# The last down projection by token tiles, with the final norm behind each tile

## The chip, the cores and the metric

The kernel runs on one core of one Trainium2 chip. The core has five engines that work side by side and wait for one another by semaphores: TensorE (PE; its weight loads are listed as PEld), VectorE (DVE), ScalarE (ACT), GpSimd (POOL) and SyncE (SP, which only issues transfers). Products are accumulated in PSUM, which has eight banks of 128 partitions by 512 float32. All else lies in SBUF. The metric is the device time of one execution in microseconds, as the median of several.

## The reference, cut to what matters

The program is a trunk of four layers over 512 tokens of width 1024. Each layer adds a mixer (S5, gated linear attention, differential attention, S5 again) and then a feed-forward part to the residual stream `x`; a last norm gives the output. The change concerns the last lines only:

```python
def rmsnorm(x, g):
    xf = x.astype(jnp.float32)
    y = xf * lax.rsqrt(jnp.mean(xf * xf, axis=-1, keepdims=True) + NORM_EPS)
    return (y * g.astype(jnp.float32)).astype(x.dtype)

def swiglu_ffn(h, w_gate_up, w_down):
    g, u = jnp.split(h @ w_gate_up, 2, axis=-1)
    return (jax.nn.silu(g) * u) @ w_down
...
        h = rmsnorm(x, norm_ffn[layer])
        x = x + swiglu_ffn(h, w_gate_up[layer], w_down[layer])
    return rmsnorm(x, norm_final)
```

The hidden width of the feed-forward part is 2816, which the kernel handles as eleven blocks of 256.

## The kernel before, in words

**Tiles.** `x` lies in SBUF as 128 partitions by four token tiles by 1024 columns. All products run in float32r, and each operand is split into a high part (a rounded copy) and a low part (the rest), so that one product of 128 x 128 by 128 x 512 is three matmuls: high by high, high by low, low by high. That is `mm3` (L394), whose three matmuls are L396, L397 and L398.

**Weights.** One panel of the down weights is 256 rows by 512 columns, 512 KB. `wb` (L388) loads it through SP's queue into one of three staging buffers `wst` (L357), ACT copies the high part into one of five split buffers `whl` (L368), and DVE writes the low part behind it (L376).

**The feed-forward part.** `ffn` (L717) works on the eleven blocks in three groups of 4, 4 and 3 (L799). For each block, gate and up products are made, gated and split into `act` (L704, L705). After each group the group's share of the down product is added to `x`. In the last group that is six row blocks k of 128 hidden columns, so three panels for each of the two column halves d.

**The down product.** `gemm_b` (L400) takes one half at a time. It opens four accumulators in PSUM (tag `acc`, four banks), one for each token tile, and goes over panels, over the two row blocks in a panel and over the four token tiles. When a tile's last k is done, `add_x` (L539) scales the bank by the token's norm factor `r` and adds it to `x` on DVE (L548). For half 1 of the last group the last four k (`tail=4`) are taken token tile by token tile, so that the four sums end one behind the other. PSUM's other four banks are two of tag `s` and two of tag `tp`, which the last group's down product does not use.

**The final norm.** `run` (L2486) ends with a loop over the token tiles. `normed` (L492) lets ACT square a tile of 1024 columns into a scratch tile `sq` and sum it along the way (L500), DVE adds epsilon (L487), POOL raises to the power -1/2 (L489), and DVE multiplies the tile by that factor and by the gain into a tile `h` (L504), which SP stores (L2508). `sq` and `h` have two buffers each and come from a pool `last`, opened when the feed-forward part's pool has been closed. The gain comes by a load on SP's queue (L480) into the one buffer of tag `gain`, which the feed-forward part lends out as a room for weights before.

**What sets the order.** A first stretch of each feed-forward part is ordered by hand (L749 to L785). From L786 on, a planner orders each engine's instructions: it goes by the order in the program and by its own estimate of when operands and buffers are ready, and it writes all waits. Within an engine the order it gave is fixed at run time. `issue_after` ties an instruction behind another one of the same engine; `gemm_b` uses it, by way of `self.behind`, so that in half 0 of a group's down product the panels behind the first are split only after the last silu on ACT and the last scaling on DVE (L367, L372, L835).

Of the kernel before, what the change touches and what calls it, by code (L numbers as in the profile page):

```python
# [11 lines left out]
F32 = mybir.dt.float32  # L12
# [3 lines left out]
AF = mybir.ActivationFunctionType  # L16
ALU = mybir.AluOpType
# [4 lines left out]
P = 128  # L22
D = 1024
SEQ = 512
NT = SEQ // P
# [14 lines left out]
class Slices:  # L40
# [5 lines left out]
    @staticmethod  # L46
    def flat(t):
        dims = "abcdef"[: len(t.shape) - 1]
        return t[:] if len(dims) == 1 else t[:].rearrange(f"p {' '.join(dims)} -> p ({' '.join(dims)})")
# [239 lines left out]
class Trunk:  # L289
# [199 lines left out]
        nc.gpsimd.tensor_tensor(r[:], v, self.mhalf[:, :n], op=ALU.pow)  # L489
        return r  # L490

    def normed(self, xt, g, out, pool, aside=False):  # L492

        nc = self.nc
        if pool is None:
            junk = self.wp.tile([P, D], F32, tag="wst", name="sq", bufs=3)
        else:
            junk = pool.tile([P, D], F32, tag="sq", name="sq", bufs=2)
        ms = self.sp.tile([P, 1], F32, tag="ms", name="ms", bufs=2)
        nc.scalar.activation(junk[:], xt, AF.Square, scale=1.0 / 32.0, accum_out=ms[:])  # L500
        r = self.rsqrt(ms[:], 1, 1e-6)
        if out is None:
            h = pool.tile([P, D], F32, tag="h", name="h", bufs=2)
            nc.vector.scalar_tensor_tensor(h[:], xt, r[:], g[:], op0=ALU.mult, op1=ALU.mult)  # L504
            return h
        if aside:
            nc.scalar.mul(junk[:], xt, r[:])
            gr = lambda y: y.rearrange("p (g c) -> p g c", c=16)
            nc.gpsimd.tensor_tensor(out, gr(junk[:]), gr(g[:]), op=ALU.mult)
            return  # L510
        nc.vector.scalar_tensor_tensor(
            out, xt.rearrange("p (g c) -> p g c", c=16), r[:],
            g[:].rearrange("p (g c) -> p g c", c=16), op0=ALU.mult, op1=ALU.mult,
        )

    def split_t(self, dst_hi, dst_lo, src):
        nc = self.nc
        nc.scalar.copy(dst_hi, src)
        nc.vector.tensor_tensor(dst_lo, src, dst_hi.bitcast(F32), op=ALU.subtract)
# [50 lines left out]
    def seven_block(self, fp, slots, left, wgu, b, turn, na):  # L570
# [143 lines left out]
            add, six, six_out, seven, seven_out, three, three_out, four, gate2, parts, four_out,  # L714
        )}

    def ffn(self, l, left, after=None, turn=False, aside=None, small=None):  # L717


        jobs = bool(aside or small)  # L720
        i = self.i
        wgu, wd = i["ffn_w_gate_up"][l], i["ffn_w_down"][l]
        nxt = None
        r = left.r
        with self.tc.tile_pool(name=f"ffn{l}", bufs=1, reuse_waits="tile") as fp:
# [13 lines left out]
            f = blocks[:2]  # L739
# [27 lines left out]
            for step in plan.split():  # L767
                name, _, n = step.partition(":")
# [12 lines left out]
                elif name == "turn":  # L781
                    r = self.turn_x(left.r) if turn else r
# [15 lines left out]
            b0 = 0  # L798
            for nb in (4, 4, 3) if na == 4 else (3, 3, 3, 2):  # L799
                acts = []  # L800
                for n in range(b0, b0 + nb):
                    b = blocks[n]
                    if n > 1:
                        for w in ("direct", "room1", "room22", "room21", "summed"):
                            b[w]()
                    if n < 2:
                        b["gate2"]()
                        continue
                    if n == 2:
                        b["one"]()  # L810
                        b["five"]()
                        b["one_out"]()
                        b["add"]("22")
                        b["split"]("1")
                        b["split"]("21")
                        acts.append(blocks[0]["parts"]())
                        acts.append(blocks[1]["parts"]())
                        b["five_out"]()
                    else:
                        for step in ("one", "one_out", "five", "five_out"):  # L820
                            b[step]()
                        b["add"]("22")
                    if n > 1:
                        for step in ("six", "six_out", "two", "two_out", "gate1", "seven", "seven_out", "three", "three_out"):
                            b[step]()
                        b["add"]("21")
                        b["four"]()
                    acts.append(b["four_out"]())
                stat = lambda k, part, t: acts[k // 2][:, part, k % 2, t * P : (t + 1) * P]
                if b0 + nb == 11 and after is not None:  # L830
                    nxt = (Chunks if turn else Left)(self, after)
                for d in range(2):
                    tail = 4 if d == 1 and b0 + nb == 11 else 0
                    self.gemm_b(stat, wd, 2 * nb, d * 512, self.add_x(d, nxt, r), k0=2 * b0, tail=tail, jobs=jobs,
                                behind=None if d else dict(self.last))  # L835
                b0 += nb
# [1340 lines left out]
    def diff(self, l, left):  # L2177
# [4 lines left out]
        with self.tc.tile_pool(name="diff", bufs=1) as p:  # L2182
# [193 lines left out]

            units = project(0, 0)
            run(units)
            tables()
            units = project(0, 1)  # L2380
            run(units)
            units = project(0, 2)
            run(units, 8)
            rest()
            prepare(0)
# [100 lines left out]
    def run(self):  # L2486
        nc, i = self.nc, self.i
        with ExitStack() as ctx:
            left = self.s5_first(ctx)

        def small():
            yield from self.diff_tables()
            yield from self.s5_phases_spilled(1)

        left = self.ffn(0, left, i["norm_mix"][1], aside=lambda fp: self.s5_spilled(fp, 1))
        left = self.gla(1, left)
        left = self.ffn(1, left, i["norm_mix"][2], small=small)
        left = self.diff(2, left)
        left = self.ffn(2, left, i["norm_mix"][3], turn=True)
        with ExitStack() as ctx:  # L2500
            left = self.s5_second(3, ctx, left)
        self.ffn(3, left)
        g = self.gain(i["norm_final"])
        o = self.out[0].rearrange("(p t) c -> p t c", t=NT)
        with self.tc.tile_pool(name="last", bufs=1, side="right") as p:
            for t in range(NT):
                h = self.normed(self.x[:, t], g, None, p)
                nc.sync.dma_start(o[:, t], h[:])  # L2508


_INS = [
# [35 lines left out]
```

## Time and profile before

| | |
|---|---|
| median of 3 runs | 2273.04 us (2271.74 to 2274.02) |
| profiled execution | 2275.95 us, its span 2274.2 us |
| TensorE busy | 2208.0 us, 97% of the span |
| DVE, ACT, POOL busy | 1560.9, 1120.4, 281.0 us |
| granted TensorE clock, mean | 0.991 |
| first matmul of the last down product | starts at 2228.24 us |
| last matmul of the program | starts at 2260.66 us |

The span runs from the first to the last instruction on the core; the profiled execution's time is a little more. Times in the timeline are microseconds from the span's start. A row of the timeline gives start, duration, engine, line, operation, output and inputs, shape, and in brackets how long the engine stood idle before it and who released it. A row of the groups by line gives count, busy time and mean nanoseconds. SPq is SP's queue of transfer issues. Matmuls overlap one another, so a matmul's own duration is longer than the step from one to the next.

### The profile page before, as it was taken

To read this page: it belongs to the slowest core of one execution; us is meant where nothing else is said; L and a number is where in the kernel's file an instruction comes from. 1 tells how busy PE (TensorE), PEld (TensorE's weight loads), DVE (VectorE), ACT (ScalarE), POOL (GpSimd) and SP (SyncE) were. 2 spreads that over 40 slices of the span, in tenths; PEclk is the share of its full clock that TensorE was granted. 3 is DMA by queue.
4 is the path that set the end of the run, shared out by engine and by line. 5 is a ranking of instruction groups with operands and counts; after the bars stand their busy time and mean duration, and the time that the engine had idled before them with its cause. 6 is when DMAs were issued, how large, how long until landed. Compare 5 with 4: busy or idle time off the path is not lost.

```text
span 2274.2 us, 37228 instructions
## 1 busy us (share of the span) xinstructions
PE 2208.0 (97%) x14847; PEld 1959.7 (86%) x14847; DVE 1560.9 (69%) x2420; ACT 1120.4 (49%) x1870; POOL 281.0 (12%) x392
## 2 busy tenths in 40 slices
PE   6999999999999999999999999999999899999997
PEld 4778989889777799998988887999998888989896
DVE  8873977776624469777744675977766964957574
ACT  6533645454453455555535676644444234635342
POOL 1000141522000010101002231101000001101000
PEclk9999999999999999999999999999999999999999
DMA  4247476663422457766336366976631646767521
GB/s 86 50 145 193 107 195 161 174 189 90 123 68 72 138 141 188 188 165 172 97 126 147 90 150 156 242 208 148 171 90 46 159 130 158 194 159 181 152 76 65
DMA packets 295463, 317.83 MB, mean 140 GB/s; under 512 B 72221, under 2 KB 235353, under 8 KB 294906
## 3 DMA queue, kind: packets, MB, share of 16 engines
q1 hardware_dynamic: 233050, 234.23, 34.3%
q0 software_dynamic: 62240, 81.22, 19.2%
q8 instruction: 117, 1.92, 0.3%
q14 instruction: 56, 0.46, 0.1%
HBM read 283.54 MB, written 16.65 MB: 132 GB/s over the span
## 4 chain that ended last, share of the span: by engine, by line
PE 81%; DVE 9%; ACT 4%; issue 2%; DMA 2%; SPq 1%; POOL 0%; ACTq 0%; DVEq 0%; POOLq 0%
PE a L565 18%; PE acc L396 13%; PE acc L398 13%; PE acc L397 13%; PE c L565 8%; PE d L565 4%; PE y L1481 2%; DVE whl L376 2%; ACT whl L368 1%; PE V L1445 1%; PE s L2309 1%; PE op L2343 1%; PE tp L123 1%; DVE halves L229 1%; ACT halves L211 1%
## 5 line engine op out<-in xcount | busy, mean ns | idle before, releaser
L376 DVE TENSOR_TENSOR whl<-wst,whl 128x1024 fp32r<-128x1024 f32 x272 | 331.8, 1224 | 262.9 <-ACT whl L368 262.3
L368 ACT CAST whl<-wst 128x1024 fp32r<-128x1024 f32 x272 | 284.0, 1050 | 312.6 <-PE acc L398 220.8
L565 PE MATMUL a<-side,whl 128*128 128x256 f32 x3168 | 383.0, 277 | 3.9 <-DVE whl L376 3.6
L565 PEld LDWEIGHTS a<-side,whl 128*128 128x128 f32 x3168 | 369.6, 188 | 6.5 <-DVE whl L376 5.5
L396 PE MATMUL acc<-whl,act 128*128 128x512 f32 x704 | 278.3, 396 | 0.8 <-DVE x L548 0.7
L397 PE MATMUL acc<-whl,act 128*128 128x512 f32 x704 | 274.7, 390 | 0.0
L398 PE MATMUL acc<-whl,act 128*128 128x512 f32 x704 | 274.6, 390 | 0.0
L565 PE MATMUL c<-side,whl 128*128 128x256 f32 x2112 | 254.7, 277 | 1.2 <-DVE whl L376 1.2
L565 PEld LDWEIGHTS c<-side,whl 128*128 128x128 f32 x2112 | 247.0, 188 | 2.0 <-DVE whl L376 2.0
L376 DVE TENSOR_TENSOR whl<-slot,whl 128x1024 fp32r<-128x1024 f32 x107 | 130.5, 1223 | 68.7 <-ACT whl L368 68.7
L396 PEld LDWEIGHTS acc<-whl,act 128*128 128x128 f32 x704 | 132.1, 188 | 31.1 <-issue 2.3
L398 PEld LDWEIGHTS acc<-whl,act 128*128 128x128 f32 x704 | 132.2, 188 | 28.1
L397 PEld LDWEIGHTS acc<-whl,act 128*128 128x128 f32 x704 | 132.2, 188 | 25.6
L368 ACT CAST whl<-slot 128x1024 fp32r<-128x1024 f32 x107 | 112.2, 1053 | 82.4 <-PE acc L398 34.1
L396 PE MATMUL acc<-whl,hT 128*128 128x512 f32 x352 | 142.8, 406 | 0.0
L398 PE MATMUL acc<-whl,hT 128*128 128x512 f32 x352 | 138.2, 393 | 0.0
L397 PE MATMUL acc<-whl,hT 128*128 128x512 f32 x352 | 138.0, 392 | 0.0
L565 PE MATMUL a<-sides,whl 128*128 128x256 f32 x1056 | 134.3, 283 | 0.0
L565 PEld LDWEIGHTS a<-sides,whl 128*128 128x128 f32 x1056 | 129.8, 191 | 0.9
L565 PE MATMUL d<-sides,whl 128*128 128x256 f32 x1056 | 126.6, 276 | 1.0 <-ACT whl L368 1.0
L565 PEld LDWEIGHTS d<-sides,whl 128*128 128x128 f32 x1056 | 122.9, 188 | 1.2 <-ACT whl L368 1.2
L704 ACT CAST act<-r 128x512 fp32r<-128x512 f32 (+1 forms) x110 | 66.3, 646 | 116.0 <-DVE r L683 108.5
(458 smaller groups left out, 3884.1 us busy)
## 6 DMA issues: line engine op xcount, KB each, us to landing
wst<-in_ffn_w_gate_up_dram SPq DMA_DIRECT2D x88, 512.0 KB, 4.9
wst<-in_ffn_w_down_dram SPq DMA_DIRECT2D x88, 512.0 KB, 4.3
slot<-in_ffn_w_gate_up_dram SPq DMA_DIRECT2D x71, 512.0 KB, 5.6
wst<-in_ffn_w_gate_up_dram POOLq DMA_DIRECT2D x44, 512.0 KB, 6.2
halves<-in_ffn_w_gate_up_dram SPq DMA_DIRECT2D x43, 512.0 KB, 5.3
wst<-in_s_w_glu_dram SPq DMA_DIRECT2D x32, 512.0 KB, 4.6
wst<-in_gla_w_in_dram SPq DMA_DIRECT2D x24, 512.0 KB, 3.8
wst<-in_diff_w_qkv_dram SPq DMA_DIRECT2D x24, 512.0 KB, 4.5
```

What stands on the lines that cost most here:

```text
L123: tr.nc.tensor.transpose(p[:, j], h[:, j * P : (j + 1) * P], tr.ident[:])
L211: self.tr.nc.scalar.mul(self.F[t // 2, d][:, j, (t % 2) * P : (t % 2 + 1) * P], p[:, j], self.gcol[:, 4 * d + j : 4 * d + j + 1])
L229: v.tensor_tensor(s, s, y, op=op)
L368: self.last["high"] = self.nc.scalar.copy(hl[:, 0], w[:])
L376: self.last["low"] = self.nc.vector.tensor_tensor(hl[:, 1], w[:], hl[:, 0].bitcast(F32), op=ALU.subtract)
L396: mm(out, lh, rh, start=first, stop=False)
L397: mm(out, lh, rl, start=False, stop=False)
L398: self.last["mm"] = mm(out, ll, rh, start=False, stop=last)
L565: mm(o, hl[:, x, k, c], side[y][:, k], start=first and not (j or k or n), stop=k == 3 and n == 2, skip_group_check=True,)
L704: self.last["act high"] = nc.scalar.copy(dst[:, 0, j], src[:, j])
L1445: mm(V[kk][z][:, bs(b)], inm[:, z, bs(b)], U[:, bs(b)], start=True, stop=True)
L1481: mm(yb[:, b], q[:, j, b], om[:, j // 2, bs(b)], start=False, stop=j == 3)
```

## The change

For the last group of the last layer (`after is None`) `ffn` calls a new function `last_down` in place of the two `gemm_b` calls, and `run` ends with `ffn(3, left)`. `normed` goes.

`last_down` asks for all eight banks: four `acc` for half 0, and two `s` and two `tp` for half 1. It asks for the gain first. Then it takes k 0 and 1 of half 0 and k 0 and 1 of half 1, each over the four token tiles. After that it asks for the four panels left, two for each half, and goes token tile by token tile: k 2 to 5 of half 0, then k 2 to 5 of half 1. Behind each half's last product the bank is added to `x` as before, and ACT squares the 512 columns of `x`, writing the squares into the bank that was just read and their sum into a column of `ms`. When both halves of a tile are there, one DVE instruction adds the two sums and epsilon, POOL takes the power, and DVE multiplies the two halves of `x` in place by the factor and the gain. Each half is stored by itself, so there are eight stores of 256 KB in place of four of 512 KB. The `behind` tie holds for the panels of both halves, but for the first panel.

```diff
+    def last_down(self, stat, wd, nk, k0, r):
+        nc = self.nc
+        v = nc.vector
+        g = self.gain(self.i["norm_final"])
+        o = self.out[0].rearrange("(p t) c -> p t c", t=NT)
+        ms = self.np_.tile([P, 2, NT], F32, tag="msq", name="msq")
+        flat = lambda y: y[:].rearrange("p a b -> p (a b)")
+        banks = [
+            [self.acc()[:] for t in range(NT)],
+            [self.sbank()[:], self.sbank()[:], flat(self.tp("last")), flat(self.tp("last"))],
+        ]
+        behind = dict(self.last)
+
+        def product(t, d, k, hl):
+            self.mm3(
+                banks[d][t], stat(k, 0, t), stat(k, 1, t), hl[:, 0, k % 2], hl[:, 1, k % 2], k == 0, k == nk - 1
+            )
+
+        for d in range(2):
+            hl = self.wb(wd, k0, d * 512)
+            self.behind = behind
+            for k in range(2):
+                for t in range(NT):
+                    product(t, d, k, hl)
+        hls = [[self.wb(wd, k0 + kb, d * 512) for kb in range(2, nk, 2)] for d in range(2)]
+        self.behind = None
+        for t in range(NT):
+            for d in range(2):
+                for k in range(2, nk):
+                    product(t, d, k, hls[d][k // 2 - 1])
+                xs = self.x[:, t, d * 512 : (d + 1) * 512]
+                v.scalar_tensor_tensor(xs, banks[d][t], r[:, t : t + 1], xs, op0=ALU.mult, op1=ALU.add)
+                nc.scalar.activation(banks[d][t], xs, AF.Square, scale=1.0 / 32.0, accum_out=ms[:, d, t : t + 1])
+            sum_ = self.sp.tile([P, 1], F32, tag="ms", name="ms", bufs=2)
+            v.tensor_scalar(sum_[:], ms[:, 0, t : t + 1], ms[:, 1, t : t + 1], 1e-6, op0=ALU.add, op1=ALU.add)
+            f = self.rsqrt(sum_[:], 1, 0.0)
+            for d in range(2):
+                cut = slice(d * 512, (d + 1) * 512)
+                xs = self.x[:, t, cut]
+                v.scalar_tensor_tensor(xs, xs, f[:], g[:, cut], op0=ALU.mult, op1=ALU.mult)
+                nc.sync.dma_start(o[:, t, cut], xs)
...
+                if b0 + nb == 11 and after is None:
+                    self.last_down(stat, wd, 2 * nb, 2 * b0, r)
+                    break
                 for d in range(2):
                     tail = 4 if d == 1 and b0 + nb == 11 else 0
                     self.gemm_b(stat, wd, 2 * nb, d * 512, self.add_x(d, nxt, r), k0=2 * b0, tail=tail, jobs=jobs,
...
         self.ffn(3, left)
-        g = self.gain(i["norm_final"])
-        o = self.out[0].rearrange("(p t) c -> p t c", t=NT)
-        with self.tc.tile_pool(name="last", bufs=1, side="right") as p:
-            for t in range(NT):
-                h = self.normed(self.x[:, t], g, None, p)
-                nc.sync.dma_start(o[:, t], h[:])
```

More of the change, by code (lines that the diff above doesn't have):

```diff
@@ L490, in rsqrt @@
         return r
[L492 to L514, printed above, removed]
     def split_t(self, dst_hi, dst_lo, src):
```

## The prediction, made before the result was known

> **What bounds the kernel now.** I read the page first, then the groups by line in the last stretch, the timeline of the end and the waits there.
>
> ```profile
> span 2274.2 us, 37228 instructions
> PE 2208.0 (97%) x14847; PEld 1959.7 (86%) x14847; DVE 1560.9 (69%) x2420; ACT 1120.4 (49%) x1870; POOL 281.0 (12%) x392
> ```
>
> TensorE sets the time nearly everywhere, so a change that leaves its products as they are can only win where TensorE has nothing left to do. The windows view shows that place: after the last product.
>
> ```profile
> 2228.40:2244.70 16.30, 16.30 (x73) 13.48 (x73) 10.00 (x12) 6.10 (x7) 0.00 (x0) 1.00 0.20 64
> 2250.20:2261.06 10.86, 10.85 (x48) 8.64 (x47) 2.25 (x3) 0.00 (x0) 0.00 (x0) 1.00 0.00 0
> 2261.06:2274.20 13.14, 0.00 (x0) 0.00 (x0) 6.24 (x9) 4.38 (x8) 2.18 (x4) 0.63 0.40 160
> ```
>
> (Columns: window, its length, busy us and instructions of PE, PEld, DVE, ACT and POOL, granted clock, DMA share, GB/s.) In the last products TensorE is full at clock 1.00 and the other engines have room: of the 10.86 us to 2261.06, DVE works 2.25 and ACT 0. Then come 13.14 us without any product. The timeline shows what fills them.
>
> ```profile
> 2228.24 0.39 PE L396 MATMUL acc<-whl,act 128*128 128x512 f32 x1
> ...
> 2260.66 0.39 PE L398 MATMUL acc<-whl,act 128*128 128x512 f32 x1
> 2261.09 0.75 DVE L548 SCALAR_TENSOR_TENSOR x<-acc,rcol,x 128x512 f32<-128x512 f32 x1 [1.97 <-PE acc L398]
> 2261.14 1.06 ACT L500 ACTIVATE sq<-x 128x1024 f32<-128x1024 f32 x1 [21.51 <-PE acc L398]
> 2262.10 0.19 ACT L500 ACTIVATION_READ_ACCUMULATOR sq<-x 128x1 f32 x1
> ...
> 2262.32 0.15 DVE L487 TENSOR_SCALAR ms<-ms 128x1 f32<-128x1 f32 x1 [0.48 <-ACT sq L500]
> 2262.56 0.56 POOL L489 TENSOR_TENSOR rs<-ms,mhalf 128x1 f32<-128x1 f32 x1 [75.01 <-DVE ms L487]
> ...
> 2263.16 1.28 DVE L504 SCALAR_TENSOR_TENSOR h<-x,rs,gain 128x1024 f32<-128x1024 f32 x1 [0.68 <-POOL rs L489]
> ...
> 2264.52 6.39 SPq L2508 DMA_DIRECT2D out_dram<-h  x4
> ...
> 2269.26 1.29 DVE L504 SCALAR_TENSOR_TENSOR h<-x,rs,gain 128x1024 f32<-128x1024 f32 x1 [0.68 <-DMA out_dram<-h]
> ```
>
> All four squares come after the last product, although tile 0 of x was complete far earlier: the first square waited 21.51 us, and its releaser is the last product, not x. Its output `sq` lies in a pool opened after the feed-forward pool, whose tiles TensorE reads to the end. Then four norms go one behind the other, and the fourth also waits 0.68 us for a store, since `h` has two buffers. The last store is issued at 2264.52 + 6.39 - 0.34 = 2270.57; from there to the end of the span are 3.63 us (the store's own view, then windows of half a us):
>
> ```profile
> L2508 SPq DMA_DIRECT2D out_dram<-h x4: 332/344/357, 2264.5 to 2270.6; - x4
> DMA to landing us min/median/max: 2.6/2.7/2.7
> ```
>
> ```profile
> 2271.00:2271.50 0.50, 0.00 (x0) 0.00 (x0) 0.00 (x0) 0.00 (x0) 0.00 (x0) 0.50 0.25 98
> 2271.50:2272.00 0.50, 0.00 (x0) 0.00 (x0) 0.00 (x0) 0.00 (x0) 0.00 (x0) 0.50 1.02 410
> 2272.00:2272.50 0.50, 0.00 (x0) 0.00 (x0) 0.00 (x0) 0.00 (x0) 0.00 (x0) 0.50 1.00 401
> 2272.50:2273.00 0.50, 0.00 (x0) 0.00 (x0) 0.00 (x0) 0.00 (x0) 0.00 (x0) 0.50 0.36 139
> ```
>
> Of these 3.63 us, 2.68 go to landing, of which some 1.3 are transfer (512 KB at about 400 GB/s), and 0.95 to the end of the program.
>
> **The change part by part. The products.** 144 matmuls before, 144 after, the same shapes and panels. From the first start to the last are 143 steps, (2260.66 - 2228.24) / 143 = 0.2267 us each. The order changes: 24 for half 0 on the first two rows of blocks (k 0 and 1), 24 for half 1, then 24 for each token tile, with 12 in a row on one bank as the old tail had already. Nothing in this costs TensorE anything if the six weight panels come in time. By the new order panel 2 (half 1) is wanted after 24 steps, at 2233.68; panel 3 after 48, at 2239.12; and then, six matmuls apart, panel 4 at 2240.48, panel 5 at 2241.84, panel 6 at 2243.20. Before, panels 5 and 6 were wanted after 96 and 102 steps, at 2250.0 and 2251.4. When they are ready:
>
> ```profile
> 2229.82 1.04 ACT L368 CAST whl<-wst 128x1024 fp32r<-128x1024 f32 x1
> 2235.88 1.05 ACT L368 CAST whl<-wst 128x1024 fp32r<-128x1024 f32 x1 [2.60 <-DMA wst<-in_ffn_w_down_dram]
> 2238.58 1.05 ACT L368 CAST whl<-wst 128x1024 fp32r<-128x1024 f32 x1 [1.65 <-DMA wst<-in_ffn_w_down_dram]
> ...
> 2230.89 1.23 DVE L376 TENSOR_TENSOR whl<-wst,whl 128x1024 fp32r<-128x1024 f32 x1 [0.25 <-ACT whl L368]
> 2232.63 2.36 DVE L376 TENSOR_TENSOR whl<-wst,whl 128x1024 fp32r<-128x1024 f32 x2
> 2236.96 1.23 DVE L376 TENSOR_TENSOR whl<-wst,whl 128x1024 fp32r<-128x1024 f32 x1 [1.97 <-ACT whl L368]
> 2239.66 1.23 DVE L376 TENSOR_TENSOR whl<-wst,whl 128x1024 fp32r<-128x1024 f32 x1 [1.48 <-ACT whl L368]
> ```
>
> Panel 2 is split by 2232.12 (1.56 us ahead), panels 3 and 4 by 2234.99, panel 5 by 2238.19 (3.65 ahead), panel 6 by 2240.89 (2.31 ahead, where it had 10.5). The loads, the three staging buffers and the five split buffers turn in the same order as before; panel 6 takes the split buffer of panel 1, which is read until 2233.7. I cost this at nothing, covered by these margins; a loss of order here is a rival below. The tie of half 1's panels behind the last silu and scaling binds only panel 2, and the second panel had that tie before. TensorE ends at 2261.05 again.
>
> **The gain.** Its request moves in the program past the six panel loads, on SP's queue.
>
> ```profile
> 2179.26 0.34 SPq L480 DMA_DIRECT2D gain<-in_norm_final_dram  x1
> 2181.98 0.37 SPq L357 DMA_DIRECT2D wst<-in_ffn_w_gate_up_dram  x1
> 2193.94 40.31 SPq L357 DMA_DIRECT2D wst<-in_ffn_w_down_dram  x6
> ```
>
> The planner had already issued it at 2179.26, ahead of all six, so nothing on that queue changes places: cost 0.
>
> **Tiles 0 to 2.** Their sums end at 2261.05 less 5.44 (24 x 0.2267) per tile: 2244.7, 2250.2, 2255.6. Each then has two adds, two squares, one sum, one power, two scalings and two stores, which is about 3.2 us of DVE, 1.6 of ACT, 0.56 of POOL and 0.7 of SP's issuing in 5.44 us of products. The products hide it. Without that cover the old cadence returns, about 2 us a tile (2263.16 to 2269.26 for three), 6.1 in all. An add of the next tile's half 0 may stand on DVE ahead of this tile's scalings; those are then later by under 1 us. What queues behind a waiting add, sum or square is only norm work once panel 6 is split, and no product waits for it, as each of the eight banks is filled once.
>
> **Tile 3, which sets the end.** The durations:
>
> ```profile
> L548 DVE SCALAR_TENSOR_TENSOR x<-acc,rcol,x 128x512 f32<-128x512 f32 x80 | 56.7, 750 | 30.8 <-PE acc L398 30.8
> L2326 DVE SCALAR_TENSOR_TENSOR pr<-pr,sums 128x512 f32<-128x512 f32 x32 | 24.0, 751 | 0.7
> L487 DVE TENSOR_SCALAR ms<-ms 128x1 f32<-128x1 f32 x4 | 0.5, 148 | 0.5 <-ACT sq L500 0.5
> L2322 DVE TENSOR_SCALAR sums<-st,sums,neglam 128x1 f32<-128x1 f32 x32 | 8.7, 273 | 0.8
> L114 ACT ACTIVATE sq<-x 128x512 f32<-128x512 f32 x40 | 25.3, 632 | 29.6 <-DVE x L1886 17.1 <-DVE x L546 9.7 <-DVE x L548 2.8
> L655 ACT COPY r<-c 128x512 f32<-128x512 f32 x44 | 26.0, 592 | 17.3 <-PE c L565 17.3
> ```
>
> Half 0 is summed 12 matmuls (2.72 us) earlier and its add and square are long done. Half 1: the add runs from 2261.09 to 2261.84. Its square follows after about 0.05; with its accumulator read the old square of 1024 columns took 2262.29 - 2261.14 = 1.15, and 512 columns take 1.049 - 0.632 = 0.42 less, so 0.73: 2262.62. The sum with one column and one constant added lies between L487's 148 ns and L2322's 273 (two columns); I take 0.21: 0.03 + 0.21 brings 2262.86. POOL starts 0.09 later and takes 0.56: 2263.51. The two scalings of 512 columns, all in SBUF and in place as in L2326, take 0.75 each, the second starting 0.07 before the first ends (four adds in a row took 2.79): 2263.55 to 2264.98. The second store is issued at about 2265.0.
>
> No row shows ACT writing PSUM. The nearest are ACT reading PSUM (592 ns) and the square in SBUF (632), so I bound it by 0.59 and 0.69 and take 0.63, nearest in form. The Trainium skill ("ScalarE: Activation LUTs", Step-by-step: what each stage is for) says that ScalarE reaches PSUM faster than SBUF; no run here shows it yet, and by it the sum would be shorter by a few hundredths.
>
> The last store carries 256 KB instead of 512, so 0.65 us less transfer at the rate above. The store ahead of it is issued 0.7 us earlier and needs 0.65, so it is out of the way. By this the last store lands after 2.68 - 0.65 = 2.03; the other bound is 2.68, nothing saved. I take 2.03, because the window rows show the transfer as a separate part. The end: 2265.0 + 2.03 + 0.95 = 2268.0.
>
> A rule speaks against the cut: the Trainium skill ("DMA: Bandwidth & Descriptors", Measured) asks for stores of 1 MiB and more, and its Anatomy of one DMA gives 2.0 us plus bytes at 436 GB/s, which is 3.2 us for 512 KB, where the trace has 2.7, and 2.6 for 256 KB. By that the end would be an estimated 2268.6 instead of 2268.0, since only the last store is in the open.
>
> **Sum.** The span goes from 2274.2 to 2268.0, 6.2 us less. Of the 13.1 us behind the last product 6.95 stay: 0.79 add, 0.78 square, 0.89 sum and power, 1.47 scalings and issue, 2.98 store and end, with 0.04 of rounding. The profiled execution took 2275.95, 1.75 more than its span, and 2.9 more than the median of the timed runs, 2273.04. I take the same 6.2 off both: 2269.75 for a profiled execution, 2266.8 for the median. With the bounds (sum 0.06 either way, square 0.06, store 0.65 worse, scalings at half of L504's 1.28, 0.2 better) the likeliest case lies between 2266.5 and 2267.6, and with the scatter of the medians (2271.74 to 2274.02 before) between 2265.5 and 2268.5.
>
> **Rivals. A: panel splits late.** The planner sets ACT's and DVE's order from its own durations. If it thinks panels 5 and 6 come late, it puts tile 0's first square ahead of their casts. Then cast 5 waits for half 0 of tile 0 (2242.0), its add (2242.8) and square (2243.6), ends at 2244.6, and the split on DVE at 2245.9: TensorE, which wants the low part at 2242.07, stands 3.8 us (2.4 if only panel 6 is behind). Gain 2.4 to 3.8; time 2270.6 at worst. For it: load 6 goes out only with the sixth issue, near 2233.9, and ACT already stood 1.65 us for it. Against it: all six panels precede every square in the program, and the margin is 2.31 us.
>
> **B: the banks cost TensorE.** Nothing but TensorE is known here to write PSUM during products. Seven of the eight squares would do so while TensorE accumulates in other banks. If each holds TensorE for the square with its read (0.82) and the restart of an empty pipe (0.39 + 0.19, a matmul and a weight load unoverlapped), that is 7 x 1.40 = 9.8 us, 3.6 more than the gain: 2276.6, slower. It decides from 6.2 / 7 = 0.89 us a square. Against it: ACT's and DVE's reads of other banks leave no gap in TensorE (the window 2228.40 to 2244.70 with four adds is full).
>
> **C: the norms don't move.** If the order on TensorE isn't kept tile by tile, or something again holds the squares to the end, the cadence of 2 us a tile stays and only the store wait and the smaller last store are saved: 13.1 - 0.7 - 0.65, so about 2271.7. Against it: the squares' place was what held them (21.51 us), and the banks are free as soon as they are read.
>
> **How the numbers follow.** Forecast 0.76, A 0.10, B 0.06, C 0.06, others 0.02, of either sign. About 0.2% (4.5 us) is what a measurement of this kernel can tell from no change, so faster needs 2268.5 or less. Faster: the forecast but for a twentieth of it, and half of the others, 0.73. Same: A, C, that twentieth and half of B, 0.23. Slower: the rest, 0.04. The range reaches from 2265.0 (forecast and scatter) to 2270.6, the end of A, and leaves out C, B and a little below.
>
> **What would show it.** The window behind the last product shrinks to about 7 us and holds one tile's norm, with a store issue near 3.95 us behind the last product; `out_dram` has eight stores of 256 KB, and the last lands in 2.0 us (step right) or 2.7 (wrong). The 144 matmuls still take 32.8 us; a gap beside panel 5 or 6 is A, a spacing above 0.2267 us under a square is B. Squares of tiles 0 to 2 still behind the last product are C and would make the prediction wrong, as would a last product later than 2261.05 by more than 2 us.

## The result, and the profile after

The changed kernel takes 2265.78 us (median of 7 runs, 2264.44 to 2268.24) against 2273.04 us (median of 7, 2271.45 to 2274.02): a ratio of 0.9971, 95% interval 0.9962 to 0.9980. That is 7.3 us less by the medians, where the prediction had 6.2 and a time of 2266.8.

The profiled execution took 2265.08 us, with a span of 2263.3 us. That is 10.9 us less than the span before, which is more than the tail can give. The timeline of the products in the last down stage shows why:

```profile
2223.33 0.39 PE L396 MATMUL acc<-whl,act 128*128 128x512 f32 x1
...
2255.76 0.39 PE L398 MATMUL last<-whl,act 128*128 128x512 f32 x1
```

The stage started at 2223.33 where it was 2228.24 before, 4.91 us earlier. Ahead of it each engine has the same instructions in the same order as before. From the first start to the last the 143 steps take 32.43 us, as they did (32.42). What is left is the tail, from the start of the last matmul to the end of the span: 2274.2 - 2260.66 = 13.54 us before, 2263.3 - 2255.76 = 7.54 us after. The change is worth 6.0 us in this profile; the 4.9 us in front of it are taken up in the first experiment.

The windows after the change (window, length, busy us and instructions of PE, PEld, DVE, ACT, POOL, granted clock, DMA share, GB/s):

```profile
2245.11:2256.15 11.04, 11.04 (x49) 8.82 (x47) 6.08 (x10) 2.93 (x9) 1.10 (x2) 1.00 0.27 102
2256.15:2263.30 7.15, 0.00 (x0) 0.00 (x0) 2.38 (x4) 0.72 (x2) 0.55 (x1) 0.76 0.20 74
```

In the last two tiles' products DVE, ACT and POOL now work 6.08, 2.93 and 1.10 us, where they had 2.25, 0 and 0 in a stretch of about that length before (10.86 us). TensorE stays full at clock 1.00. Behind the last product there is one tile's norm. The timeline of the end on DVE, ACT, POOL and SP's queue:

```profile
2256.19 0.75 DVE L726 SCALAR_TENSOR_TENSOR x<-last,rcol,x 128x512 f32<-128x512 f32 x1 [0.94 <-PE last L398]
2257.72 0.21 DVE L729 TENSOR_SCALAR ms<-msq 128x1 f32<-128x1 f32 x1 [0.79 <-ACT last L727]
2258.60 1.42 DVE L734 SCALAR_TENSOR_TENSOR x<-x,rs,gain 128x512 f32<-128x512 f32 x2 [0.66 <-POOL rs L489]
...
2256.97 0.60 ACT L727 ACTIVATE last<-x 128x512 f32<-128x512 f32 x1 [0.97 <-DVE x L726]
2257.51 0.19 ACT L727 ACTIVATION_READ_ACCUMULATOR last<-x 128x1 f32 x1
...
2258.02 0.55 POOL L489 TENSOR_TENSOR rs<-ms,mhalf 128x1 f32<-128x1 f32 x1 [4.89 <-DVE ms L729]
...
2243.08 17.29 SPq L735 DMA_DIRECT2D out_dram<-x  x8
```

The stores' own view:

```profile
L735 SPq DMA_DIRECT2D out_dram<-x x8: 332/332/356, 2243.1 to 2260.0; - x8
DMA to landing us min/median/max: 2.0/2.1/2.1
```

The last store is issued at 2243.08 + 17.29 - 0.33 = 2260.04, which is 4.28 us behind the start of the last matmul. It lands 2.0 us later, and 1.3 us follow to the end of the span. The same view of the last store alone gives 2.6 us before the change, which leaves 1.0 us to the end there.

### The profile page after: what moved, and what is told of

It reads as the page before. It is cut to its first block, busy times and chain, and to the rows that moved or that the text cites. A ratio compares the mean times of both kernels' runs of the same rounds, so it can differ in the third digit from the quotient of the medians.

```text
span 2263.3 us, 37243 instructions
## 1 busy us (share of the span) xinstructions
PE 2200.7 (97%) x14847; PEld 1952.7 (86%) x14847; DVE 1561.8 (69%) x2424; ACT 1121.4 (50%) x1878; POOL 281.2 (12%) x392
## 4 chain that ended last, share of the span: by engine, by line
PE 83%; DVE 8%; ACT 4%; issue 2%; DMA 1%; SPq 1%; POOL 0%; ACTq 0%; DVEq 0%; POOLq 0%
PE a L541 18%; PE acc L396 14%; PE acc L398 13%; PE acc L397 13%; PE c L541 8%; PE d L541 4%; PE y L1504 2%; DVE whl L376 2%; ACT whl L368 1%; PE V L1468 1%; PE op L2366 1%; PE s L2332 1%; PE tp L123 1%; DVE halves L229 1%; ACT halves L211 1%
## 5 line engine op out<-in xcount | busy, mean ns | idle before, releaser
L396 PE MATMUL acc<-whl,act 128*128 128x512 f32 x680 | 268.9, 396 | 1.9 <-DVE x L524 1.9
L397 PE MATMUL acc<-whl,act 128*128 128x512 f32 x680 | 265.3, 390 | 0.0
L398 PE MATMUL acc<-whl,act 128*128 128x512 f32 x680 | 265.3, 390 | 0.0
L396 PEld LDWEIGHTS acc<-whl,act 128*128 128x128 f32 x680 | 127.6, 188 | 31.3 <-issue 2.7
L398 PEld LDWEIGHTS acc<-whl,act 128*128 128x128 f32 x680 | 127.7, 188 | 27.0
L397 PEld LDWEIGHTS acc<-whl,act 128*128 128x128 f32 x680 | 127.7, 188 | 24.7
```

The lines of the kernel that those rows point to most:

```text
L396: mm(out, lh, rh, start=first, stop=False)
L397: mm(out, lh, rl, start=False, stop=False)
L398: self.last["mm"] = mm(out, ll, rh, start=False, stop=last)
```

## The experiments

The tail (start of the last matmul to the end of the span) can be read to about 0.1 us in a profile, the medians to about 1 us. So the verdicts on fractions of a us rest on the tail. The ratios compare with the kernel before on the same chip.

### Both kernels once more

No edit. For the changed kernel the expectation was:

> The changed kernel once more, unchanged. The tail, from the start of the last matmul to the end of the span, was 13.54 us before and 7.54 us after; the first product of the last down stage started at 2228.24 us before and at 2223.33 us after, 4.91 us earlier, although nothing ahead of it was changed. Theory S (scatter): the 4.91 us belong to the one execution, most of them to the first 90 us; this profile starts the stage anywhere between 2222 and 2229, the tail is 7.5 +- 0.1 again, and the ratio of the medians is 1 - 6.0/2273 = 0.9974 within 0.0010. Rival P (placement): the change also made the stretch ahead faster; then the stage starts again within 0.5 us of 2223.3 and the ratio is near 1 - 10.9/2273 = 0.9952.

and for the kernel before:

> The kernel before, unchanged, for one more profile. Theory S (scatter ahead of the last stage): the stage's first product starts between 2222 and 2229 us, not necessarily at 2228.24, with a tail of 13.5 +- 0.1 us. Rival P (the change sped up what lies ahead of it): the start is within 0.5 us of 2228.2.

The changed kernel gave 2266.94 us, ratio 0.9977 (0.9968 to 0.9986). Its profile:

```profile
2229.06 0.39 PE L396 MATMUL acc<-whl,act 128*128 128x512 f32 x1
...
2261.49 0.39 PE L398 MATMUL last<-whl,act 128*128 128x512 f32 x1
```

The tail is 2269.1 - 2261.49 = 7.61 us, and the stage starts at 2229.06, later than before the change. The kernel before, profiled again, starts the stage at 2228.35, with a tail of 2274.3 - 2260.78 = 13.52 us. That start alone fits both theories; but rival P falls with the changed kernel's two profiles, whose starts are 5.7 us apart. Over all profiles here the start lies between 2222.3 and 2229.1 us. The spread stands early in the execution already, as one and the same load on POOL's queue shows, in the first and the second profile of the changed kernel:

```profile
201.49 1.30 POOL L577 DMA_DIRECT2D lent<-in_ffn_w_gate_up_dram  x1 [59.35 <-PE acc L398]
```

```profile
205.09 1.30 POOL L577 DMA_DIRECT2D lent<-in_ffn_w_gate_up_dram  x1 [58.76 <-PE acc L398]
```

By then 3.6 of the 5.7 us are there. So the 4.9 us lie within the scatter of single executions of one kernel, and the effect of the change is the tail's 5.9 to 6.0 us. Both ratios hold that value (1 - 6.0/2273 = 0.9974).

### The old order of the products

```diff
-        for d in range(2):
-            hl = self.wb(wd, k0, d * 512)
...
-        for t in range(NT):
-            for d in range(2):
-                for k in range(2, nk):
-                    product(t, d, k, hls[d][k // 2 - 1])
...
+        for kb in range(0, nk, 2):
+            hl = self.wb(wd, k0 + kb, 0)
+            self.behind = behind
+            for k in range(kb, kb + 2):
+                for t in range(NT):
+                    product(t, 0, k, hl)
+                    if k == nk - 1:
+                        added(t, 0)
...
+        hls = [self.wb(wd, k0 + kb, 512) for kb in range(2, nk, 2)]
+        for t in range(NT):
+            for k in range(2, nk):
+                product(t, 1, k, hls[k // 2 - 1])
+            added(t, 1)
```

(`added` is the add to `x` and the square into the bank, as after the change.)

> Half 0 is multiplied to its end for all tiles, then half 1, as before the change; squares into the banks, scaling in place and eight stores as after it. Token tiles then end 2.72 us apart instead of 5.44. Theory 'place' (what gained is that the squares no longer wait for the space of the feed-forward part): most of the gain stays. By DVE's order in this kernel each add of the next tile stands behind the scalings of this one, so it slips by about 1.1 us a tile, and tile 3's sum stands behind tile 2's scalings; I work out a tail of 9.4 us (8.5 to 10.4), 1.9 more than after, a ratio to before near 0.998. Rival 'order' (the gain comes from finishing whole tiles one by one): tail 12 us or more, ratio 0.999 to 1.000. If DVE could keep up, 7.5 us and 0.9974.

Measured: 2267.99 us, ratio 0.9978 (0.9969 to 0.9987); tail 2265.2 - 2255.98 = 9.22 us. DVE's timeline at the end:

```profile
2255.77 0.75 DVE L715 SCALAR_TENSOR_TENSOR x<-last,rcol,x 128x512 f32<-128x512 f32 x1
2257.31 0.21 DVE L737 TENSOR_SCALAR ms<-msq 128x1 f32<-128x1 f32 x1 [0.79 <-ACT last L716]
2257.44 0.74 DVE L715 SCALAR_TENSOR_TENSOR x<-last,rcol,x 128x512 f32<-128x512 f32 x1
2258.19 1.42 DVE L742 SCALAR_TENSOR_TENSOR x<-x,rs,gain 128x512 f32<-128x512 f32 x2
2259.52 0.21 DVE L737 TENSOR_SCALAR ms<-msq 128x1 f32<-128x1 f32 x1
2260.39 1.42 DVE L742 SCALAR_TENSOR_TENSOR x<-x,rs,gain 128x512 f32<-128x512 f32 x2 [0.66 <-POOL rs L489]
```

With tiles ending every 2.72 us, tile 3's add (2257.44) stands behind tile 2's sum, and its own sum (2259.52) behind tile 2's scalings. That is 1.6 to 1.7 us more than after the change. Taking whole tiles through both halves gives DVE 5.44 us a tile and is worth this much; the rest of the gain, some 4.3 us, came without it. The theory 'place' gets its 9.4 almost exactly, and 'order' (12 or more) falls as the source of the whole gain.

### The squares' place alone

Two kernels with the same program: products and adds as after the change, and the whole norm in a loop behind the feed-forward part, where the old one stood. They differ in one operand.

```diff
         for t in range(NT):
             for d in range(2):
                 xs = self.x[:, t, d * 512 : (d + 1) * 512]
-                junk = banks[d][t]
+                junk = pool.tile([P, 512], F32, tag="sq", name="sq", bufs=4)[:]
                 nc.scalar.activation(junk, xs, AF.Square, scale=1.0 / 32.0, accum_out=ms[:, d, t : t + 1])
...
         rest = self.ffn(3, left)
         with self.tc.tile_pool(name="last", bufs=1, side="right") as p:
             self.last_norm(*rest, p)
```

(The line with minus is that of the run with banks, the one with plus that of the run with the scratch tile.)

> Products and adds as after the change, but the squares go to a scratch tile of 512 columns from a pool opened when the feed-forward pool is closed, as before the change, and the norm loop stands in the program behind all adds; scaling in place and half stores as after. Theory 'place': the first square starts only after the last product (0.5 us behind its start), tiles follow one another every 2.3 us through DVE, POOL and ACT, and the tail is 13 to 14.5 us: the whole gain of 6.0 us is lost, ratio to before 0.999 to 1.001. Rival 'order' (finishing whole tiles, scaling in place and smaller stores bring it): tail 9 us or less, ratio 0.998 or less.

> The same program as the run with the scratch tile, the norm loop behind all adds, but the squares go into the banks. It differs from that run in the squares' place alone. Theory 'place': the squares of tiles 0 to 2 move behind TensorE again, tail 7.5 to 7.7 us, ratio near 0.9974. Rival (the place in the program holds the norms back, not the space): tail 13 us or more, as with the scratch tile.

With the scratch tile: 2274.07 us, ratio 1.0002 (0.9993 to 1.0011), tail 2272.4 - 2258.26 = 14.14 us. With the banks: 2265.81 us, ratio 0.9976 (0.9965 to 0.9986), tail 2265.9 - 2258.28 = 7.62 us. The waits with the scratch tile and, in the second fence, with the banks (engine and line, who they waited for, us in total, times, longest):

```profile
ACT sq L737 <- PE last L398: 21.3, 1, 21.3
```

```profile
ACT acc L737 <- DVE x L726: 12.0, 4, 3.0
```

In the scratch tile the first square waits 21.3 us for the last product, as the kernel before did (21.51); in the banks each waits for its own add (the row shown is that of the four `acc` banks; those of the other four name the same releaser). DVE with the scratch tile:

```profile
2261.00 1.42 DVE L744 SCALAR_TENSOR_TENSOR x<-x,rs,gain 128x512 f32<-128x512 f32 x2 [0.69 <-POOL rs L489]
2262.33 0.21 DVE L739 TENSOR_SCALAR ms<-msq 128x1 f32<-128x1 f32 x1
2263.22 1.41 DVE L744 SCALAR_TENSOR_TENSOR x<-x,rs,gain 128x512 f32<-128x512 f32 x2 [0.68 <-POOL rs L489]
...
2267.62 1.42 DVE L744 SCALAR_TENSOR_TENSOR x<-x,rs,gain 128x512 f32<-128x512 f32 x2 [0.67 <-POOL rs L489]
```

The four tiles follow one another every 2.2 us, since each tile's sum stands behind the scalings of the one before and then waits for POOL. So the gain hangs on the place of the squares: with the squares in the old space the eight banks, the order by tiles, scaling in place and half stores together bring nothing, and the tail is even 0.6 us longer than before. The place in the program makes no difference here (7.62 us against 7.54 to 7.61). Whether moving the squares alone would have been enough in the kernel before is not shown: its scaled tile `h` comes from the same pool as `sq`, so its scalings might have waited too, and no run keeps `h` there with the squares moved.

### Squares into SBUF that is free

```diff
-                nc.scalar.activation(banks[d][t], xs, AF.Square, scale=1.0 / 32.0, accum_out=ms[:, d, t : t + 1])
+                junk = self.np_.tile([P, 512], F32, tag="h", name="sq", bufs=2)
+                nc.scalar.activation(junk[:], xs, AF.Square, scale=1.0 / 32.0, accum_out=ms[:, d, t : t + 1])
```

> The changed kernel with the squares written to a 512-column tile in SBUF that is free in time, not into the banks. Theory 'place': only the wait matters, not that it is PSUM: the square takes 0.63 instead of 0.60 us, the tail 7.55 to 7.65 us, the ratio near 0.9974. If writing PSUM costs TensorE anything, the 143 steps of the last down stage, 32.43 us after the change, get shorter here, by 0.2 us or more; I expect 32.43 +- 0.03. Rival: freeing SBUF of scratch is what brings the gain; then the tail is 13 us.

Measured: 2266.61 us, ratio 0.9971 (0.9958 to 0.9984), tail 2266.0 - 2258.40 = 7.60 us, 143 steps in 32.43 us. The groups by line and form on ACT, here and, in the second fence, after the change:

```profile
L728 ACT ACTIVATE sq<-x 128x512 f32<-128x512 f32 x8 | 5.1, 632 | 17.3 <-DVE x L726 17.3
```

```profile
L727 ACT ACTIVATE acc<-x 128x512 f32<-128x512 f32 x4 | 2.4, 602 | 11.8 <-DVE x L726 11.8
```

A square into a bank takes 602 ns, into SBUF 632. On this the Trainium skill ("ScalarE: Activation LUTs", Step-by-step: what each stage is for), which says that ScalarE reaches PSUM faster, and the trace agree, at 30 ns. And it costs TensorE nothing: its 143 steps are the same to 0.01 us with and without it. Both kinds of space that were free in time do, PSUM and SBUF.

### Whole stores

```diff
                 v.scalar_tensor_tensor(xs, xs, f[:], g[:, cut], op0=ALU.mult, op1=ALU.mult)
-                nc.sync.dma_start(o[:, t, cut], xs)
+            nc.sync.dma_start(o[:, t], self.x[:, t])
```

> The changed kernel with one store of 512 KB per tile behind both scalings, four in all. By the transfer term of the prediction the last store lands 2.65 us behind its issue instead of 2.05, so the tail is 8.1 to 8.2 us, 0.6 more. If only a fixed cost counted the tail would stay at 7.55; if the first half's store were in the way of the second now, it would be shorter than 7.5.

Measured: 2267.83 us, ratio 0.9975 (0.9964 to 0.9986), tail 2266.1 - 2258.17 = 7.93 us: 0.3 to 0.4 us more than with half stores, not 0.6. The stores' view:

```profile
L735 SPq DMA_DIRECT2D out_dram<-x x4: 332/344/357, 2246.2 to 2262.5; - x4
DMA to landing us min/median/max: 2.6/2.7/2.7
```

The landing term is as priced: the last store lands 2.6 us behind its issue, against 2.0. The difference sits behind it. From the last landing to the end of the span 1.0 us go by here and before the change, and 1.3 us in the changed kernel. The trace shows what fills the rest. At its end SP's queue goes through a row of semaphore checks, some 0.06 us apart, and among them are the semaphores of the stores. From the last landing to the end of that row there are, here and, in the second fence, after the change:

```profile
L2560 SPq EVENT_SEMAPHORE  x3: 28/28/28, 2265.1 to 2265.2; - x3
```

```profile
L2560 SPq EVENT_SEMAPHORE  x7: 28/28/28, 2262.1 to 2262.4; - x7
```

The semaphore of the last of four stores stands late in the row, that of the last of eight stands early, so four more checks are left when the changed kernel's last store lands: 4 x 0.06 = 0.24 us. The size of the store plays no part in this. No run tries another order of the checks.

### Panels 5 and 6 tied behind a square

```diff
-        hls = [[self.wb(wd, k0 + kb, d * 512) for kb in range(2, nk, 2)] for d in range(2)]
+        hls = [[self.wb(wd, k0 + kb, 0) for kb in range(2, nk, 2)]]
...
+                if len(hls) < 2:
+                    with self.tc.issue_after(sq.ins):
+                        hls.append([self.wb(wd, k0 + kb, 512) for kb in range(2, nk, 2)])
```

(`sq` is the square of tile 0's half 0, the first one on ACT.)

> The changed kernel with the splits of panels 5 and 6 tied behind tile 0's first square on ACT, which is rival A made real. By the prediction's price TensorE stands 3.8 us: the 143 steps take 36.2 us. But the planner knows of the tie and now takes tile 1's half 0 (12 matmuls, 2.72 us) ahead of tile 0's half 1, which fills most of the gap: I work out panel 5's high part at 16.3 us and its low part at 17.6 us behind the first product, against 16.3 us of products that are ready, so 0.3 to 1.3 us of standing, 32.7 to 33.7 us for the 143 steps, and an unchanged tail of 7.5 us.

Measured: 2267.46 us, ratio 0.9970 (0.9959 to 0.9981), 143 steps in 2261.65 - 2228.97 = 32.68 us, tail 7.55 us. TensorE lost 0.25 us, just under the 0.3 of the expectation's lower end. Its timeline where panel 5 is wanted:

```profile
2245.08 0.39 PE L398 MATMUL acc<-whl,act 128*128 128x512 f32 x1
2245.30 0.71 PE L396 MATMUL sb<-whl,act 128*128 128x512 f32 x2
2245.85 0.39 PE L396 MATMUL acc<-whl,act 128*128 128x512 f32 x1
2246.08 0.40 PE L397 MATMUL acc<-whl,act 128*128 128x512 f32 x1
2246.32 0.39 PE L398 MATMUL acc<-whl,act 128*128 128x512 f32 x1
2246.55 0.50 PE L397 MATMUL sb<-whl,act 128*128 128x512 f32 x1
```

The planner has put tile 1's half 0 ahead, starts half 1 with the high part alone, and fills the time to the low part with three matmuls of another tile.

### The two last scalings side by side

```diff
+                if d == 0:
+                    gx = self.np_.tile([P, 512], F32, tag="h", name="gx", bufs=2)
+                    v.tensor_tensor(gx[:], xs, g[:, :512], op=ALU.mult)
...
-            for d in range(2):
-                cut = slice(d * 512, (d + 1) * 512)
-                xs = self.x[:, t, cut]
-                v.scalar_tensor_tensor(xs, xs, f[:], g[:, cut], op0=ALU.mult, op1=ALU.mult)
-                nc.sync.dma_start(o[:, t, cut], xs)
+            nc.scalar.mul(self.x[:, t, :512], gx[:], f[:])
+            nc.scalar.dma_start(o[:, t, :512], self.x[:, t, :512])
+            xs = self.x[:, t, 512:]
+            v.scalar_tensor_tensor(xs, xs, f[:], g[:, 512:], op0=ALU.mult, op1=ALU.mult)
+            nc.sync.dma_start(o[:, t, 512:], xs)
```

> The changed kernel with the last two scalings of a tile side by side: DVE multiplies half 0 by the gain ahead of time (0.69 us, behind its add, while TensorE works), and behind the power ACT multiplies that by the factor (0.69 us) and stores it through its own queue, while DVE does half 1 as before (0.75 us). Behind the power 0.75 us remain in place of 1.42, so the last store is issued 0.67 us earlier: the tail goes from 7.54 to 7.61 us in the runs so far to 6.9 to 7.0 us. In the time that is 0.03%, which the medians can't show; the ratio to before is 0.997 +- 0.001. If the store through ACT's queue lands later than SP's 2.05 us, or the end waits longer for two queues, the gain in the tail is smaller; if both together cost over 0.6 us, it is none.

Measured: 2266.72 us, ratio 0.9975 (0.9963 to 0.9986), tail 2262.5 - 2254.73 = 7.77 us, 0.2 us longer than after the change. The timeline of DVE and ACT shows the two scalings side by side, and the second fence the stores' view:

```profile
2257.57 0.75 DVE L737 SCALAR_TENSOR_TENSOR x<-x,rs,gain 128x512 f32<-128x512 f32 x1 [0.66 <-POOL rs L489]
...
2257.57 0.72 ACT L734 ACTIVATE x<-gx,rs 128x512 f32<-128x512 f32 x1 [0.91 <-POOL rs L489]
2258.32 0.37 ACTq L735 DMA_DIRECT2D out_dram<-x  x1
```

```profile
L735 ACTq DMA_DIRECT2D out_dram<-x x4: 349/368/403, 2242.0 to 2258.3; - x4
L738 SPq DMA_DIRECT2D out_dram<-x x4: 332/344/356, 2242.1 to 2258.4; - x4
...
DMA to landing us min/median/max: 2.6/2.8/3.1
```

Both halves are now issued within 0.1 us, the first at 2258.32 - 2254.73 = 3.59 us behind the start of the last matmul, where the last store after the change was issued at 4.28. The six landings that the profile has of the eight stores lie 2.6 to 3.1 us behind their issue, as long as for one store of 512 KB or longer. The windows of the last two transfers and of the time behind them, here and, in the second fence, after the change, show where the 0.6 us went:

```profile
2259.18:2260.70 1.52, 0.00 (x0) 0.00 (x0) 0.00 (x0) 0.00 (x0) 0.00 (x0) 0.50 0.92 345
2260.70:2262.50 1.80, 0.00 (x0) 0.00 (x0) 0.00 (x0) 0.00 (x0) 0.00 (x0) 0.50 0.00 0
```

```profile
2260.21:2261.72 1.51, 0.00 (x0) 0.00 (x0) 0.00 (x0) 0.00 (x0) 0.00 (x0) 0.50 0.93 346
2261.72:2263.30 1.58, 0.00 (x0) 0.00 (x0) 0.00 (x0) 0.00 (x0) 0.00 (x0) 0.50 0.00 0
```

In both the two halves move in 1.5 us at about 345 GB/s, and the transfer ends 2260.70 - 2254.73 = 5.97 us behind the start of the last matmul here and 2261.72 - 2255.76 = 5.96 us after the change. Half stores 0.7 us apart took that transfer in turn; issued together they share it and end no earlier. So the 0.6 us won on the engines is given back in the transfer, and the 0.2 us lost come behind it (1.80 against 1.58 us). No version here beats the changed kernel.

## Why the prediction was right, step by step

**The bound.** The view that mattered was the idle stretch behind the last product and the 21.51 us wait of the first square. That the wait came from the scratch tile's space was read from one row; the pair of kernels that differ in this operand shows it.

**The products** at no cost: right, 32.43 us for the 143 steps against 32.42. **Panels**: split by 2233.39 (panel 5) and 2236.52 (panel 6) in the profile after, wanted at 2236.9 and 2238.3, so 3.5 and 1.8 us ahead, where 3.65 and 2.31 were worked out. The rows (of DVE, the last two splits):

```profile
2232.17 1.22 DVE L376 TENSOR_TENSOR whl<-wst,whl 128x1024 fp32r<-128x1024 f32 x1 [2.08 <-ACT whl L368]
2235.29 1.23 DVE L376 TENSOR_TENSOR whl<-wst,whl 128x1024 fp32r<-128x1024 f32 x1 [1.90 <-ACT whl L368]
```

**The gain** on SP's queue: right, issued ahead of all six panels as before.

**Tile 3.** From the start of the last matmul to the end of the scalings 4.32 us were forecast and 4.26 measured; add 0.75, square 0.60 for 0.63, sum 0.21, power 0.55, scalings 1.42 for 1.43. The landing of the last store was forecast at 2.03 and took 2.0. Here the trace goes against the estimate of 2.6 us for 256 KB by the formula of the Trainium skill ("DMA: Bandwidth & Descriptors", Anatomy of one DMA), which the page fits to DMAs issued from GpSimd; these stores go by SP's queue. The one term that was mis-sized is the end of the program. The prediction took the median landing of all stores, 2.68 us, for the last one, which left 0.95; the last store itself took 2.6, which leaves 1.0, and 1.3 are measured after the change, because four more semaphore checks stand behind its landing. So the tail is 7.54 to 7.61 us for 7.34 forecast, and the gain 5.9 to 6.0 for 6.2. The medians' 7.3 and 5.9 us lie on both sides of it: the median of 2265.78 us lies 1.0 below the forecast, but the tail shows no better step, so that is put down to scatter. The range reaches down to 2265.0 where the sum has 2265.5, without a reason; the result lies inside either.

**Rival A** (late panels) had a wrong price: 3.8 us were worked out with TensorE's order held fixed, and 0.25 us were measured with both panels tied behind the square. The planner moved other products into the gap. **Rival B** (banks cost TensorE): nothing, against 9.8 us. **Rival C** (the norms stay behind): the scratch tile makes it happen, with a tail of 14.14 us where C had 12.2. What C had wrong is the cadence: it kept the old 2.0 us a tile, less 0.7 for the store wait, and the tiles came every 2.2 us and began with two squares in a row; the end of 1.3 us adds the last 0.3.

## What to carry to other kernels

When an engine off the critical path waits for the busiest one although its operands are long ready, look at where its output lies: a scratch tile in space that another stage still reads is a dependency like any other, and moving the scratch can be worth more than reordering work. Put post-processing behind parts of a result only as fine as the slowest engine of the chain can follow: at 2.72 us a tile DVE's queue made the last tile wait for the one before, at 5.44 us it did not. And at the end of a program two engines that finish together can give back through the shared transfer what they won.

## What the runs showed that was not expected

Two stores of 256 KB issued together from two queues land in 2.6 to 3.1 us each, against 2.0 for the second of two issued 0.7 us apart on one queue. The end of the program takes 1.0 or 1.3 us behind the last landing, by how many of the 0.06 us checks on SP's queue stand behind that of the last store. And profiles of kernels whose instructions ahead of the last stage are the same start that stage up to 6.8 us apart (2222.3 to 2229.1), more than the whole effect. Of the 5.7 us between the changed kernel's two profiles 3.6 are there after 200 us, but of the 6.8 between the extremes only 1.75 (the load shown above starts at 203.34 in the run with the scalings side by side, at 205.09 in the second profile of the changed kernel). What causes it stays open, so a difference of two spans is no measure of a change of this size.
